# A decoder trunk's first output projection: its first pair of chunks with a quarter of the contraction in seven products

## The chip, the cores and the metric

The kernel runs on one core of one Trainium2 chip. The metric is the device time of one execution in microseconds: the median of 3 runs is 1020.32 us (1020.16 to 1020.44).

The engines are named as in the profile: PE is TensorE (matmuls), PEld its loading of the stationary operand, DVE is VectorE, ACT is ScalarE, POOL is GpSimd, SP is SyncE. SP and POOL issue the DMAs that matter here, each in the order of its own queue. A name with q behind it (SPq, POOLq) is the engine's instruction queue.

## The reference

Two layers over 256 positions of 2048 features in fp32. The first layer runs two token mixers side by side and projects their gated outputs back to 2048 features. That projection is the subject:

```python
ya = hgrn2(...)
ya = head_rmsnorm(ya, a_norm[j]) * jax.nn.silu(za.astype(jnp.float32))
xc = causal_conv(xb, b_conv_w[j], b_conv_b[j])
yb = rg_lru(xc, ...)
yb = yb * jax.nn.silu(zb.astype(jnp.float32))
y = jnp.concatenate([ya, yb], axis=-1).astype(h.dtype)
mix = y @ e_w_out[j]
...
h = h + mix
pl = rmsnorm(p[i].astype(h.dtype) @ ple_w[i], ple_norm[i])
h = h + jax.nn.sigmoid(h @ ple_gate_w[i]) * pl
```

y is 256 x 2048 and e_w_out is 2048 x 2048.

## The kernel before

**Products.** Every large product is made in three matmuls. Weights are loaded in blocks of 128 x 1024 floats (512 KB), and each block is split into a high part (a cast on ACT to fp32r, L137 or L221) and a low part (a subtraction on DVE, L138 or L222). Activations are split the same way. One step of 128 features of the contraction is then hi by hi, hi by lo and lo by hi, each a matmul of 128 x 128 against 128 x 512. The two halves of the positions (128 each, called hf) have a PSUM bank each.

**Chunks and quarters.** A projection's 2048 output features are cut into four chunks of 512, and the contraction into four quarters (kq) of 512. One quarter of one chunk is two weight blocks and 24 matmuls, 12 for each half. `quarter_tok` does this straight. In the first output projection (weights `a["eo"]`), `project_two` makes chunks 0 and 1 side by side in the order (chunk, quarter) (0,0) (0,1) (1,0) (1,1) (0,2) (1,2) (0,3) (1,3), in four banks.

**Seven products.** `seven` makes a pair of chunks, with one quarter of the contraction as a two by two product of blocks in seven products (Strassen's scheme in Winograd's form): products over half a quarter, 6 matmuls each, instead of eight. It needs four combinations of activations (`combos`, kept in tiles q4 and named 1 to 4), and combinations of weight blocks. These come about in three tiles: X (chunk 0, first half of the quarter), Y (chunk 1, second half) and Z (chunk 0, second half), to which the fourth block (chunk 1, first half) is added. With `acc` the fourth block is added by accumulating DMAs from POOL's queue (`add_loaded`): into X once X has been split, into Y once Y has been split and added to X. Without it the block is loaded once and DVE adds it. Banks A and F collect the halves of the first chunk, E and B those of the second; two partial sums, b5 and g, lie in SBUF. The order is a string: digits are products, a and b a straight quarter of the first or second chunk (`plain`), a dot a `pump` of waiting side work, A and F hand a half on. Products 1 and 3 (X straight, Y with combination 4) stood ahead of the string. The second pair of this projection (chunks 2 and 3) is made with `seven` in the order a5a6.2aA7b.4F.bb, without `acc`.

**Buffers.** Straight blocks go through a ring of five tiles `raw`, the split parts through four pairs whi and wlo, so a cast waits until the matmuls of the split four earlier are done. X, Y and the partial sums of a pair lie in a pool of the stage: the mixers' pool is `m0`, and pool `e0` takes its place in memory when `m0_scope.close()` is called. Before, that is after the first half of chunk 0 has been handed on (`mixed`). Anything in e0 waits for the last use of what lay in m0.

**Side work.** y comes in eight tiles, two for each quarter, by generators: `feature_major` for the first half of the features, `gated_mix` for the second, of which the last comes from the last gate chunk (weights `ew`, chunk 7). A gate chunk is transposed on DVE (L699), written to DRAM and read back in another order by POOL's queue (`across`, tiles dzb and r), and then multiplied with the mixer's output (L1048) and split. `before(kq)` runs such a generator to its end ahead of the quarter that needs it. The residual h (tiles hq) is loaded by POOL's queue; `out_proj` adds each half of a chunk to it (L604).

**Order.** The program text and priorities given to some instructions set the order on each engine when the kernel is built. Each engine runs its own list in order and waits on semaphores.

## Time and profile before

| | |
|---|---|
| median of 3 runs | 1020.32 us (1020.16 to 1020.44) |
| time of the profiled execution | 1020.23 us |
| its span in the profile | 1018.4 us |
| mean granted TensorE clock | 0.998 |
| last gate chunk ends, first output projection begins on PE | 300.01 us from the span's start |
| its second pair of chunks begins on PE | 343.53 us |

The span is the part of the execution that the profile covers; 1.8 us of the execution lie around it. Times in the profile are counted from the span's start. A group of instructions is one line, engine, operation and kind of tile, as in `L222 DVE TENSOR_TENSOR wlo<-ch,whi`, and a row of the timeline gives start, duration, engine, line, operation, tiles and count; what stands in brackets is the engine's idle time just before and what ended it. A matmul's modelled duration, 0.39 us, reaches over its successor's start, so the distance of two starts is what one matmul costs.

### The profile page before, as it was taken

The numbers are of one execution on the slowest core, as the hardware profiler recorded it, in microseconds if no ns is written. First come the engines' busy times: TensorE is split into PE (matmuls) and PEld (weight loads), VectorE is DVE, ScalarE is ACT, GpSimd is POOL, SyncE is SP. The second block draws the span as 40 slices with busy tenths as digits, with TensorE's granted clock in tenths as the row PEclk, the third lists the DMA queues.
The fourth block names the chain that finished last, engine by engine and source line by source line (L and its number), as shares of the span: only waits on it lengthen the run. The fifth ranks groups of instructions, "written<-read, shape, count | busy, mean of one in ns | idle before, by whom it ended". The sixth has DMA issues, their size and how long they took to land.

```text
span 1018.4 us, 14515 instructions
## 1 busy us (share of the span) xinstructions
PE 1009.4 (99%) x5158; PEld 838.1 (82%) x5158; DVE 842.8 (83%) x1234; ACT 661.4 (65%) x949; POOL 101.3 (10%) x182
## 2 busy tenths in 40 slices
PE   9999999999999999999999999999999999999996
PEld 8888888888888888888888888888888888888886
DVE  7858969969687887898669997888889997999794
ACT  7675554686875554666557877776676777466562
POOL 0111101011111112021011100000011110102000
PEclk9999999999999999999999999999999999999999
DMA  9987756567778799487798757567879889696852
GB/s 364 330 233 240 225 177 197 166 204 225 251 235 305 238 315 291 155 284 249 258 337 250 228 166 227 166 208 201 256 193 283 233 249 356 181 288 217 279 186 83
DMA packets 69816, 242.66 MB, mean 238 GB/s; under 512 B 9040, under 2 KB 10448, under 8 KB 69744
## 3 DMA queue, kind: packets, MB, share of 16 engines
q1 hardware_dynamic: 56016, 198.08, 58.7%
q0 software_dynamic: 13296, 43.13, 16.1%
q8 instruction: 40, 0.66, 0.3%
q10 hardware_dynamic: 432, 0.52, 0.1%
q14 instruction: 32, 0.26, 0.1%
HBM read 221.78 MB, written 19.92 MB: 237 GB/s over the span
## 4 chain that ended last, share of the span: by engine, by line
PE 99%; ACT 0%; DMA 0%; issue 0%; DVE 0%; ACTq 0%; POOLq 0%
PE mm L235 29%; PE mm L211 14%; PE mm L212 14%; PE mm L213 14%; PE mx L235 8%; PE mx L211 3%; PE mx L212 3%; PE mx L213 3%; PE mm L517 1%; PE nu L1349 1%; PE mx L517 1%; PE mm L1562 1%; PE mm L1561 1%; PE mm L1563 1%; PE st L213 1%; PE st L235 1%
## 5 line engine op out<-in xcount | busy, mean ns | idle before, releaser
L137 ACT CAST whi<-raw 128x1024 fp32r<-128x1024 f32 (+1 forms) x309 | 322.6, 1047 | 211.3 <-PE mm L213 95.2
L138 DVE TENSOR_TENSOR wlo<-raw,whi 128x1024 fp32r<-128x1024 f32 (+1 forms) x309 | 371.6, 1213 | 104.0 <-ACT whi L137 97.8
L211 PE MATMUL mm<-whi,ahl 128*128 128x512 f32 x640 | 250.5, 392 | 0.0
L212 PE MATMUL mm<-wlo,ahl 128*128 128x512 f32 x640 | 249.4, 390 | 0.0
L213 PE MATMUL mm<-whi,ahl 128*128 128x512 f32 x640 | 249.3, 389 | 0.0
L235 PE MATMUL mm<-whi,ahl 128*128 128x512 f32 x720 | 231.8, 390 | 0.0
L235 PEld LDWEIGHTS mm<-whi,ahl 128*128 128x128 f32 x720 | 135.2, 188 | 27.9
L211 PEld LDWEIGHTS mm<-whi,ahl 128*128 128x128 f32 x640 | 120.2, 188 | 25.5 <-issue 0.4
L213 PEld LDWEIGHTS mm<-whi,ahl 128*128 128x128 f32 x640 | 120.2, 188 | 25.1
L235 PE MATMUL mm<-wlo,ahl 128*128 128x512 f32 x360 | 140.5, 390 | 0.0
L212 PEld LDWEIGHTS mm<-wlo,ahl 128*128 128x128 f32 x640 | 120.2, 188 | 24.3
L222 DVE TENSOR_TENSOR wlo<-ch,whi 128x1024 fp32r<-128x1024 f32 x67 | 81.1, 1221 | 12.5 <-ACT whi L221 11.1
L221 ACT CAST whi<-ch 128x1024 fp32r<-128x1024 f32 x67 | 70.1, 1050 | 26.8 <-PE mm L235 13.8
L235 PEld LDWEIGHTS mm<-wlo,ahl 128*128 128x128 f32 x360 | 67.6, 188 | 14.1 <-DVE wlo L222 0.3
L235 PE MATMUL mx<-whi,ahl 128*128 128x512 f32 x192 | 63.3, 390 | 0.0
L212 PE MATMUL mx<-wlo,ahl 128*128 128x512 f32 x128 | 49.8, 389 | 0.0
L213 PE MATMUL mx<-whi,ahl 128*128 128x512 f32 x128 | 49.8, 389 | 0.0
L211 PE MATMUL mx<-whi,ahl 128*128 128x512 f32 x128 | 49.8, 389 | 0.0
L235 PE MATMUL mm<-whi,q 128*128 128x512 f32 x144 | 49.1, 391 | 0.0
L235 PEld LDWEIGHTS mx<-whi,ahl 128*128 128x128 f32 x192 | 36.1, 188 | 7.9 <-ACT xr L575 0.4
L235 PE MATMUL mx<-wlo,ahl 128*128 128x512 f32 x96 | 37.4, 390 | 0.0
L235 PEld LDWEIGHTS mm<-whi,q 128*128 128x128 f32 x144 | 27.0, 188 | 5.7
(389 smaller groups left out, 1318.5 us busy)
## 6 DMA issues: line engine op xcount, KB each, us to landing
raw<-in_ew_dram SPq DMA_DIRECT2D x64, 512.0 KB, 5.2
raw<-in_g_dram SPq DMA_DIRECT2D x60, 512.0 KB, 4.5
raw<-in_oqk_dram SPq DMA_DIRECT2D x32, 512.0 KB, 5.5
raw<-in_eo_dram SPq DMA_DIRECT2D x30, 512.0 KB, 5.1
raw<-in_oo_dram SPq DMA_DIRECT2D x30, 512.0 KB, 6.4
raw<-in_ov_dram SPq DMA_DIRECT2D x29, 512.0 KB, 4.2
raw<-in_oog_dram SPq DMA_DIRECT2D x24, 512.0 KB, 4.1
raw<-in_oz_dram SPq DMA_DIRECT2D x20, 512.0 KB, 5.1
```

The lines of the kernel that those rows point to most:

```text
L137: last["act"] = s.copy(h, r).ins
L138: last["dve"] = v.tensor_tensor(out=l, in0=r, in1=h.bitcast(F32), op=ALU.subtract).ins
L211: te.matmul(ps[hf], xh, wh, start=(k == 0), stop=False, skip_group_check=True)
L212: te.matmul(ps[hf], xh, wl, start=False, stop=False, skip_group_check=True)
L213: last["pe"] = te.matmul(ps[hf], xl, wh, start=False, stop=(k == KT - 1), skip_group_check=True).ins
L221: last["act"] = s.copy(hi, r).ins
L222: last["dve"] = v.tensor_tensor(out=lo, in0=r, in1=hi.bitcast(F32), op=ALU.subtract).ins
L235: last["pe"] = te.matmul(o, x, y, start=(first and k + i == 0), stop=(end and k == n - 1 and i == 2), skip_group_check=True).ins
L517: last["pe"] = te.matmul(ps[hf][:, o:o + w_], tokens(pact[x], k, hf), (hi, lo)[y][:, k * 512 + o:k * 512 + o + w_], start=(n == mine[0]), ...
L1349: te.matmul(ps[:, 0:n], x[:, i, o:o + P], y[:, b, i], start=(b == 0 and x is sh and y is vh), stop=(b == hf and y is vl))
L1561: te.matmul(o, xh, wh, start=(k == 0), stop=False)
L1562: te.matmul(o, xh, wl, start=False, stop=False)
```

## The change

The first pair of the first output projection (chunks 0 and 1) goes through `seven` instead of `project_two`, with the order 3a5a6.27ba4AF.bb and with `acc`. The combinations of the first quarter are started before the last two gate chunks instead of at the projection's start, and the same q4 tiles serve both pairs. X and Y of the first pair take tiles of m0 (tag f) and the partial sums another (tag q); m0 is closed, and e0 opened, when the first pair is through. Product 3 becomes a letter of the order strings, and so does the third chunk's quarter of another stage (c); the orders of all other stages stay as they were. The new function `moved` has no caller.

```diff
-ORDERS = {1: "a5a6.2aA7b.4F.bb", 2: "a5.2aA64.7F.bb"}
-LATE = "a526.a7b4aAF.bb"
+ORDERS = {1: "3a5a6.2aA7b.4F.bb", 2: "3a5.2aA64.7F.bb"}
+LATE = "c3a526.a7b4aAF.bb"
...
-    def two_and_seven(w, act, before, where, places, home=None, begin=None):
-
-        qs = {}
-        start("combos", combos(act, 0, qs, *where))
-        for c, ps in enumerate(project_two(w, act, before)):
-            for hf in range(2):
-                yield c, hf, ps[hf]
+    def two_and_seven(w, act, before, where, places, home=None, begin=None, first=None, qs=None):
+
+        if first is not None:
+            drain("combos")
+            yield from seven(w, 0, act, qs, (0,), *first(), order="3a5a6.27ba4AF.bb", acc=True, before=before)
+        else:
+            qs = {}
+            start("combos", combos(act, 0, qs, *where))
+            for c, ps in enumerate(project_two(w, act, before)):
+                for hf in range(2):
+                    yield c, hf, ps[hf]
         drain("combos")
         if begin is not None:
             begin()
...
-        if third is not None:
-            plain(w, j + 2, kqs[0], act, third, (True, True))
-        Y = load(room, 1, 1)
-        product(E, combo(4), split(Y), home is None)
-        W = X
-        if not acc:
-            W = load(ring, 1, 0)
-            add(Y, W)
-            add(W, X)
         did = set()
         for op in order or ORDERS[len(kqs)]:
-            if op in "ab":
+            if op == "c":
+                plain(w, j + 2, kqs[0], act, third, (True, True))
+            elif op == "3":
+                Y = load(room, 1, 1)
+                product(E, combo(4), split(Y), home is None)
+                W = X
+                if not acc:
+                    W = load(ring, 1, 0)
+                    add(Y, W)
+                    add(W, X)
+            elif op in "ab":
...
             combine()
+        qsy = {}
+        start("combos", combos(y, 0, qsy, ap, "ahl"))
         for g in range(2):
             ps = project_tok(ew, 6 + g, acth)
...
     def mixed():
-        for c, hf, src in two_and_seven(a["eo"], y, ready(y, "fm"), (ap, "ahl"), in_e0):
+        for c, hf, src in two_and_seven(a["eo"], y, ready(y, "fm"), None, in_e0, None, in_m0_end, in_m0, qsy):
             if hf == 0 and c in (1, 2):
                 load_hq(c + 1, last["hop"])
-            if (c, hf) == (0, 0):
-                m0_scope.close()
-                pe0.append(l0.enter_context(tc.tile_pool(name="e0", bufs=1)))
             yield c, hf, src
+
+    def in_m0():
+        return (lambda: m0.tile([P, 1024], F32, name="ch", tag="f"),
+                pieces(m0.tile([P, 1536], F32, name="pr", tag="q")[:, 0:1024]))
+
+    def in_m0_end():
+        m0_scope.close()
+        pe0.append(l0.enter_context(tc.tile_pool(name="e0", bufs=1)))
```

POOL's queue from the last gate chunk's way through DRAM on, before. dzb1 is that chunk in DRAM and r its way back, hq the residual, wg a tile of the later stage, dfe0 the way of chunk 0's result:

```order
L686 DMA dzb1_3051<-w_3047 128x1024
L689 DMA r_3050<-dzb1_3051 32x4x256 x4
L1111 DMA hq_3057<-in_x_dram 128x2x512
L1111 DMA hq_3059<-in_x_dram 128x2x512
L1141 MEMSET wg_3777 128x512
L686 DMA dfe0_3363<-w_3359 128x1024
```

The same queue now. ch_3082 is X of the first pair and ch_3097 its Y:

```order
L331 DMA ch_3082<-in_eo_dram 128x1024
L704 DMA dzb1_3067<-w_3063 128x1024
L707 DMA r_3066<-dzb1_3067 32x4x256 x4
L1131 DMA hq_3073<-in_x_dram 128x2x512
L1131 DMA hq_3075<-in_x_dram 128x2x512
L331 DMA ch_3097<-in_eo_dram 128x1024
L704 DMA dfe0_3338<-w_3334 128x1024
```

Two accumulating DMAs are new: the one into X stands ahead of the gate chunk's way through DRAM, the one into Y behind it and behind both loads of the residual.

SP's queue around the first loads of the second pair, before, with the semaphores that each waits for (DMAHW and DMASW are transfers issued by SP and by POOL, DVE and PE the engines). ch_3424 and ch_3438 are X and Y of the second pair, in e0:

```order
L134 DMA raw_3375<-in_eo_dram 128x1024 [waits DMAHW0_49,DVE_49]
L297 DMA raw_3450<-in_eo_dram 128x1024 [waits DMAHW1_49,DVE_49]
L297 DMA ch_3424<-in_eo_dram 128x1024 [waits DVE_49,PE_49]
L297 DMA ch_3438<-in_eo_dram 128x1024
L134 DMA raw_3454<-in_eo_dram 128x1024 [waits DMAHW2_49,DVE_49]
L134 DMA raw_3460<-in_eo_dram 128x1024 [waits DMAHW3_49,DVE_49]
```

The same place now; X and Y of the second pair are ch_3440 and ch_3454:

```order
L134 DMA raw_3386<-in_eo_dram 128x1024 [waits DMAHW7_49,DVE_49]
L314 DMA raw_3466<-in_eo_dram 128x1024 [waits DMAHW0_49,DVE_49]
L134 DMA raw_3470<-in_eo_dram 128x1024 [waits DMAHW1_49,DVE_49]
L134 DMA raw_3476<-in_eo_dram 128x1024 [waits DMAHW2_49,DVE_49]
L134 DMA raw_3518<-in_eo_dram 128x1024 [waits DMAHW3_49,DVE_49]
L134 DMA raw_3524<-in_eo_dram 128x1024 [waits DMAHW4_49,DVE_49]
L314 DMA ch_3440<-in_eo_dram 128x1024 [waits DMASW6_49,DVE_49,PE_49]
L314 DMA ch_3454<-in_eo_dram 128x1024
L1164 DMA gr_3791<-in_ogf_dram 128x256
L314 DMA raw_3575<-in_eo_dram 128x1024 [waits DMAHW6_49,DMAHW5_49,DVE_49]
```

X and Y of the second pair moved behind four blocks of the second pair's straight quarters. X's load now also waits for a transfer of POOL's queue, the accumulation into the first pair's Y, and the DVE instruction that it waits for is another: before it was the last multiply of `gated_mix`, now it is the sum of the residual with the first half of chunk 1 in `out_proj`, which reads the partial sum g in m0.

More of the change, by code (lines that the diff above doesn't have):

```diff
@@ L247, in plain, with moved, known @@
                 pump()
+    def moved(qs, kq, pool, tag):
+        for q, names in qs["tiles", kq]:
+            t = pool.tile([P, 1024], F32R, name="q4", tag=tag)
+            s.copy(t, q.bitcast(F32))
+            known(qs, kq, t, names)
+            yield
+    def known(qs, kq, q, names):
+        for n, name in enumerate(names):
+            qs[name, kq] = [[q[:, i * 512 + n * T + k * P:i * 512 + n * T + (k + 1) * P] for k in range(2)]
+                            for i in range(2)]
     def combos(act, kq, qs, pool, tag, bufs=None, offset=0):
@@ L268, in keep @@
                 v.tensor_tensor(out=q[:, 512:1024], in0=c, in1=q[:, 0:512].bitcast(F32), op=ALU.subtract)
-            for n, name in enumerate(names):
-                qs[name, kq] = [[q[:, i * 512 + n * T + k * P:i * 512 + n * T + (k + 1) * P] for k in range(2)]
-                                for i in range(2)]
+            known(qs, kq, q, names)
+            qs.setdefault(("tiles", kq), []).append((q, names))
         while 2 * kq + 1 not in act:
```

## The prediction

> **What bounds the kernel now.** I read the page first, then the stage that the change touches in a table of windows, then who issues what there on each queue.
>
> ```profile
> span 1018.4 us, 14515 instructions
> PE 1009.4 (99%) x5158; PEld 838.1 (82%) x5158; DVE 842.8 (83%) x1234; ACT 661.4 (65%) x949; POOL 101.3 (10%) x182
> ...
> PE 99%; ACT 0%; DMA 0%; issue 0%; DVE 0%; ACTq 0%; POOLq 0%
> ```
>
> TensorE is the chain: 99% of it, and no other engine has a share. A matmul taken away is gained, and any wait of TensorE is paid in full, since nothing later is idle to absorb it. The windows of the first output projection (columns: busy us and instructions of PE, PEld, DVE, ACT, POOL, then clock, DMA share, GB/s) say the same:
>
> ```profile
> 264.00:272.00 8.00, 8.00 (x40) 6.74 (x39) 3.50 (x3) 7.96 (x16) 2.19 (x4) 1.00 0.62 188
> ...
> 304.00:312.00 8.00, 8.00 (x37) 6.63 (x36) 7.19 (x11) 5.47 (x7) 3.41 (x6) 1.00 0.83 279
> 312.00:320.00 8.00, 8.00 (x37) 6.61 (x36) 4.87 (x6) 2.92 (x4) 0.76 (x2) 1.00 1.01 325
> ```
>
> TensorE is busy 8.00 us of 8 with the full clock, while the DMA engines are at their limit around 312 to 320. So the question is whether the new order of work keeps TensorE fed.
>
> **What is taken away.** The timeline of TensorE gives the first matmul of this projection and the first one of its second pair:
>
> ```profile
> 300.01 0.39 PE L211 MATMUL mm<-whi,ahl 128*128 128x512 f32 x1
> ...
> 343.53 0.39 PE L235 MATMUL mm<-whi,ahl 128*128 128x512 f32 x1
> ```
>
> Between them lie 192 matmuls (two chunks, four quarters, 24 each), so one takes 43.52 / 192 = 0.2267 us. In the changed first pair one quarter goes as seven products of 6 instead of 48 matmuls: 6 fewer, **-1.36 us**. If TensorE stayed fed the pair would end at 300.01 + 186 x 0.2267 = 342.18.
>
> **What costs nothing.** A split is a cast on ACT and a subtraction on DVE, in the page's groups (count, then busy us and mean ns):
>
> ```profile
> L222 DVE TENSOR_TENSOR wlo<-ch,whi 128x1024 fp32r<-128x1024 f32 x67 | 81.1, 1221 | 12.5 <-ACT whi L221 11.1
> L221 ACT CAST whi<-ch 128x1024 fp32r<-128x1024 f32 x67 | 70.1, 1050 | 26.8 <-PE mm L235 13.8
> ```
>
> Three more splits, two sums of the same shape on DVE (I take 1.2 us each) and seven copies and sums of banks come into a stage where ACT and DVE have room: they are busy 2.92 and 4.87 us of 8 in the window 312 to 320. Without that room they would cost up to 8 us, DVE's share. The combinations, moved up by some 30 us, add to DVE where it has 3.50 us of 8; ACT, full there, gets two short casts. A cast leads its matmuls by several us, which covers this: the timeline shows one that had to wait 3.02 us for a weight buffer.
>
> ```profile
> 293.41 1.05 ACT L137 CAST whi<-raw 128x1024 fp32r<-128x1024 f32 x1 [3.02 <-PE mm L213]
> ...
> 294.49 2.59 DVE L138 TENSOR_TENSOR wlo<-raw,whi 128x1024 fp32r<-128x1024 f32 x2 [1.60 <-ACT whi L137]
> ```
> ```profile
> ch<-in_ov_dram POOLq DMA_DIRECT2D x2, 512.0 KB, 6.6
> ```
>
> That cast is now the one of the first tile, X, whose split is done near 296. The accumulation into X stands on POOL's queue ahead of the last gate's bounce and can go then; POOL idles 15.32 us before 304.60 (below), so it delays nobody. X is needed again after 36 matmuls, at 308.2; 296 plus 6.6 us as in the same step of in_ov plus a split of 2.3 us is 304.9, hidden by 3 us.
>
> **The first new wait: the second accumulation.** The seven-product order of this pair is 3 a 5 a 6 2 7: product 7 comes after 78 matmuls, at 300.01 + 78 x 0.2267 = 317.69. It needs tile Y with the second chunk's weights accumulated into it, by a DMA on POOL's queue. That DMA now stands behind the last gate's bounce to DRAM, its four reads back and two loads of the residual. From before:
>
> ```profile
> 301.51 0.69 DVE L1099 SCALAR_TENSOR_TENSOR u<-th,u 128x512 f32<-128x512 f32 x1 [0.18 <-ACT u L1098]
> ...
> 303.59 0.70 DVE L699 STREAM_TRANSPOSE w<-u 128x512 f32<-128x512 f32 x1
> ```
> ```profile
> 304.60 0.56 POOL L686 DMA_DIRECT2D dzb<-w  x1 [15.32 <-DVE w L699]
> 309.15 2.18 POOL L689 DMA_DIRECT2D r<-dzb  x4 [3.99 <-DMA dzb<-w]
> 311.32 1.44 POOL L1111 DMA_DIRECT2D hq<-in_x_dram  x2
> ```
>
> The transpose waited behind a combination and a split; the combinations are gone from there now, so it can follow the gate's product at once: 302.9. The bounce goes out 0.3 us later (304.29 to 304.60), the reads 4.55 us after it, then 2.18 and 1.44 us of issuing: the accumulation is issued near **311.4**. How long it takes to land is not shown for this place; the nearest rows are:
>
> ```profile
> hq<-in_x_dram POOLq DMA_DIRECT2D x4, 512.0 KB, 9.0
> ```
> ```profile
> DMA to landing us min/median/max: 5.5/6.8/10.0
> ```
>
> The second row is that of the eight accumulations of in_oz on this queue, the same size. I take 9.0, since it goes third in a row of 512 KB transfers while the DMA engines are full: landed at 320.4. A cast of 1.05 us and a subtraction of 1.22 us, with 0.1 us ahead of the cast, follow, so the second matmul of product 7 (the first that needs the low part) runs at 322.8 instead of 317.9: **+4.9 us**. With 5.5 us to landing it is 1.4, with 10.0 it is 5.9. Queued behind it on TensorE is everything; DVE and ACT, in order, hold the next splits behind Y's.
>
> **The second new wait: the first load of the second pair.** Its X lies in pool e0, which lies where m0 lay. Before, m0 was closed after the first chunk and its last reader was the multiply with tt:
>
> ```profile
> 324.20 1.29 DVE L1048 TENSOR_TENSOR xr<-r,tt 128x512 f32<-128x512 f32 x2
> ```
> ```profile
> 325.56 0.81 SPq L297 DMA_DIRECT2D ch<-in_eo_dram  x2
> ```
>
> It ends at 325.49 and the load goes 0.07 us later, 18 us ahead of its use at 343.53. Now the first pair's own X, Y and partial sums lie in m0, and m0 closes when the pair is through; the load waits for the last of them, the residual's sum with the partial sum of chunk 1. That sum needs bank E, whose last matmul stands only 12 from the pair's end, at 339.46 (plus the first wait). The same step at the end of before's second pair shows the latencies:
>
> ```profile
> 382.97 0.39 PE L235 MATMUL mm<-whi,ahl 128*128 128x512 f32 x1
> ```
> ```profile
> 383.28 0.68 DVE L318 TENSOR_TENSOR pr<-mx,pr 128x512 f32<-128x512 f32 x1
> 383.88 0.68 DVE L253 TENSOR_TENSOR xr<-ahl 128x512 f32<-128x512 f32 x1
> 384.48 0.69 DVE L604 TENSOR_TENSOR hq<-pr,hq 128x512 f32<-128x512 f32 x1
> ```
>
> E's sum starts 0.31 us after the bank is done (339.77), the next DVE step 0.60 later (340.37), ends at 341.06; SP issues at 341.2. The landing of exactly this load:
>
> ```profile
> DMA to landing us min/median/max: 4.4/5.2/6.0
> ```
>
> With 5.2 it lands at 346.4, is cast by 347.55 and split by 348.8; the second matmul runs at 348.85 instead of 342.41: **+6.4 us** (5.6 to 7.3). Then Y's split, two sums and the splits of the next quarter queue on DVE at 1.15 us each, five of them within 12 matmuls: by that row the fifth is late by 0.5 us (0 to 1), **+0.5 us**. On SP behind the waiting load stand Y, a small load and Z and the later quarters; the two quarters used first are ahead of it, so nothing else starves.
>
> **The clock.** Before has no stop of TensorE, so no row shows one inside. Its end does:
>
> ```profile
> 1010.04 0.28 PE L1563 MATMUL mm<-whi,ahl 128*128 128x256 f32 x1
> ```
> ```profile
> 1012.00:1013.00 1.00, 0.00 (x0) 0.00 (x0) 0.78 (x6) 0.50 (x4) 0.00 (x0) 1.00 0.00 0
> 1013.00:1014.00 1.00, 0.00 (x0) 0.00 (x0) 1.00 (x4) 0.72 (x1) 0.00 (x0) 0.69 0.00 0
> 1014.00:1015.00 1.00, 0.00 (x0) 0.00 (x0) 0.41 (x2) 0.51 (x1) 0.00 (x0) 0.50 0.74 256
> ```
>
> The granted clock (last column but two) goes to 0.50 near 1013.4, 3.1 us after the last matmul. Both new stops are longer (3.8 us and 5.3 us to their first matmul). How long the clock then stays down no row shows; I take as long as it took to fall, 3.1 us at half speed, 1.55 us lost each time, an estimate, with 0 as the lower end, and count it for one stop of the two: **+1.55 us**. [...]
>
> **The sum.** Profiled execution 1020.23 (span 1018.4 and 1.8 around it, 0.09 below the median 1020.32, which I neglect): 1020.23 - 1.36 + 4.9 + 6.4 + 0.5 + 1.55 = 1032.2, said as **1032 us**, slower.
>
> **The rivals.**
> - Both stops, and the clock falls in both: + 1.55, 1033.8. For it: both are longer than 3.1 us. Against: one fall alone is seen, and the first stop is longer by only 0.7 us.
> - Both stops with the clock held: 1030.7.
> - Only the second stop: the accumulation lands 5 us earlier than I say, within 4 us of issue, or it is issued earlier. 5.5 us is the shortest that its like took, which still leaves 1.4 us. Then 1020.23 - 1.36 + 6.9 = 1025.8, up to 1027.3 with the clock.
> - Only the first stop: X of the second pair is not held by m0. For it: its address is that of the first pair's Y, not of the partial sums. Against: before, it waited for a tile elsewhere in m0. 1023.8, to 1025.3.
> - The other side, not slower: both waits are hidden, and six matmuls are all that changes: 1018.9, faster by 0.13%, which is no difference that a measurement of this kernel can tell (about 0.2%). The point at which this decides is the issue of two DMAs: the accumulation before some 306, and the second pair's first load before some 334. Nothing in the queues lets either go so early.
> - The change doesn't do what it says: excluded as far as the program shows, since the pair has 186 matmuls.
> - A third stop: the pieces of y for the third quarter come late, now that they are needed after 42 matmuls, at 309.5, instead of after 96. In before the last of them was made at 312.7:
>
> ```profile
> 287.09 2.18 POOL L689 DMA_DIRECT2D r<-dzb  x4 [4.16 <-ACT xr L717]
> ```
> ```profile
> 312.00 0.68 DVE L152 TENSOR_TENSOR ahl<-xr,ahl 128x512 fp32r<-128x512 f32 x1
> ```
>   Against: its data were read back from 287.09 on and there by some 297, and DVE merely took it late. Late by 1 to 3 us: to 1035.
>
> **How the numbers follow.** One stop's clock counted with both stops 0.34; both clocks 0.18; none 0.15; only the second stop 0.17; only the first 0.06; neither 0.05; a third stop besides 0.05. Likeliest 1032. The low end takes 1.4 and 5.6 us with no clock and no queueing (1025.9) and so holds the case without the first stop; the high end 5.9, 7.3, 1.0 and twice 1.55 (1036.2): 1025.5 to 1037. That leaves out the case of no wait, part of the first-only case, and the worst of the third stop. Slower by over 0.2% 0.94, within 0.2% 0.05, faster 0.01.
>
> **What would show it.** In the changed profile, TensorE's chain should lose share to two places: a wait of some 4 to 5 us before product 7 near 318 for Y's cast, with POOL's accumulation issued near 311; and one of 5 to 6 us before the second pair's first product near 347, with SP's load issued some 1 us before the first pair's last matmul. The granted clock should be below 1.00 in the few us behind at least one of them. The prediction is wrong if POOL's accumulation is issued before 306, if SP's load goes before the first pair's last 24 matmuls, or if TensorE shows no idle time above 1 us between 300 and 360.

## The result, and the profile after

| | before | after |
|---|---|---|
| median of the runs, us | 1020.38 (6 runs, 1019.86 to 1022.35) | 1039.1 (6 runs, 1037.93 to 1040.5) |
| ratio to before | 1 | 1.0182, 95% interval 1.0169 to 1.0195 |
| the profiled execution, its span, us | 1020.23, 1018.4 | 1039.82, 1038.0 |
| mean granted clock | 0.998 | 0.991 |

The change makes the kernel slower by 18.7 us. The prediction had the sign and two of the places, but 7 us too little: 1032, and the time lies above its range. Medians are over all runs and ratios over the fast ones, and only e17_four below and the kernel before beside it had one slow run each (1121 and 2636 us). The page of the changed kernel answers to the first rows shown of before:

```profile
span 1038.0 us, 14524 instructions
PE 1014.5 (98%) x5152; PEld 839.9 (81%) x5152; DVE 851.7 (82%) x1242; ACT 665.2 (64%) x956; POOL 103.3 (10%) x184
...
PE 93%; DMA 3%; ACT 1%; DVE 1%; issue 1%; POOL 0%; ACTq 0%; POOLq 0%; SPq 0%; DVEq 0%
```

TensorE's share of the chain fell from 99% to 93%; a DMA now has 3%, most of it loads of `in_eo`. TensorE is busy for 5 us longer with six matmuls fewer, which is for the most part the clock (5.3 us, below). The list of TensorE's waits names what ended them (total us, times, longest):

```profile
PE mm L239 <- ACT whi L225: 9.7, 2, 5.1
PE mm L239 <- ACT mm L362: 2.1, 1, 2.1
PE mm L239 <- DVE wlo L226: 1.2, 2, 0.8
```

The prediction had two stops; there are three. Their rows in TensorE's timeline, each behind the last matmul ahead of it or, for the second, alone (its last matmul ahead starts at 321.03):

```profile
302.84 0.39 PE L239 MATMUL mx<-whi,q 128*128 128x512 f32 x1
305.30 0.50 PE L239 MATMUL mm<-whi,ahl 128*128 128x512 f32 x1 [2.07 <-ACT mm L362]
...
307.75 0.50 PE L239 MATMUL mm<-wlo,ahl 128*128 128x512 f32 x1 [0.57 <-DVE wlo L138]
...
326.48 0.79 PE L239 MATMUL mm<-whi,q 128*128 128x512 f32 x1 [5.06 <-ACT whi L225]
327.74 0.80 PE L239 MATMUL mm<-wlo,q 128*128 128x512 f32 x1 [0.47 <-DVE wlo L226]
...
354.11 0.39 PE L239 MATMUL mm<-whi,ahl 128*128 128x512 f32 x1
359.14 0.50 PE L239 MATMUL mm<-whi,ahl 128*128 128x512 f32 x1 [4.65 <-ACT whi L225]
360.40 0.80 PE L239 MATMUL mm<-wlo,ahl 128*128 128x512 f32 x1 [0.76 <-DVE wlo L226]
```

A matmul fed follows the one ahead by 0.227 us. So the first stop costs 305.30 - 302.84 - 0.23 = 2.2 us and 0.7 more at 307.75; the second, to the low part, 327.74 - 321.49 = 6.25; the third 360.40 - 354.57 = 5.83. Then the granted clock, in windows of 1 us (the last column but two):

```profile
325.00:326.00 1.00, 0.00 (x0) 0.00 (x0) 0.00 (x0) 0.62 (x1) 0.00 (x0) 0.81 0.00 0
...
332.00:333.00 1.00, 1.00 (x5) 0.78 (x5) 1.00 (x2) 0.00 (x0) 0.00 (x0) 0.78 0.81 279
...
359.00:360.00 1.00, 0.50 (x1) 0.19 (x1) 0.87 (x1) 0.09 (x1) 0.00 (x0) 0.88 1.15 208
...
366.00:367.00 1.00, 1.00 (x4) 0.76 (x4) 1.00 (x2) 0.00 (x0) 1.00 (x3) 0.71 0.62 234
```

It is 0.50 from 325.6 to 332.4 and from 359.8 to 366.6, each 6.8 us. Between the low parts and the return of the clock 12 and 15 matmuls take 5.02 and 6.40 us instead of 2.72 and 3.40: 2.3 and 3.0 us lost. The account of the 19.6 us between the two spans:

| | us |
|---|---|
| the projection starts later (300.35 instead of 300.01, from the kernel's first loads) | +0.3 |
| six matmuls fewer | -1.4 |
| first stop, at the pair's start | +2.9 |
| second stop, product 7 | +6.25 |
| third stop, the second pair's start | +5.8 |
| half clock behind the second and the third | +2.3 + 3.0 |
| sum | 19.2 |

What stood ahead of the first stop shows in the rows of SP, DVE and ACT:

```profile
288.38 2.29 DVE L1056 TENSOR_TENSOR_SCAN tt<-av,it 128x1024 f32<-128x1024 f32 x1
290.74 0.33 SPq L314 DMA_DIRECT2D ch<-in_eo_dram  x1
298.51 1.05 ACT L225 CAST whi<-ch 128x1024 fp32r<-128x1024 f32 x1 [3.71 <-DMA ch<-in_eo_dram]
...
301.39 0.69 ACT L1117 ACTIVATE th<-mm,rth 128x512 f32<-128x512 f32 x1
...
304.64 0.61 ACT L362 COPY mm<-mm 128x512 f32<-128x512 f32 x1
```

Y lies where the scan's operand lay, so its load goes out at 290.74, behind the scan, and lands 7.7 us later. ACT works in order and stands 3.71 us idle in front of Y's cast; behind it stand the last gate's tanh (297.49 before, 301.39 now) and the copy of bank A to bank F, without which TensorE may not go on in F at 303.07. The second stop's rows: the accumulation was issued at 315.57, not 311.4, and landed near 325.3.

```profile
315.57 0.94 POOL L331 DMA_DIRECT2D ch<-in_eo_dram  x1
325.38 1.04 ACT L225 CAST whi<-ch 128x1024 fp32r<-128x1024 f32 x1 [3.93 <-DMA ch<-in_eo_dram]
```

The third's: the last reader of the first pool ends at 353.23, SP issues at once, X lands some 4.7 us later.

```profile
352.54 0.69 DVE L622 TENSOR_TENSOR hq<-pr,hq 128x512 f32<-128x512 f32 x1
353.29 0.80 SPq L314 DMA_DIRECT2D ch<-in_eo_dram  x2
358.05 1.04 ACT L225 CAST whi<-ch 128x1024 fp32r<-128x1024 f32 x1 [13.34 <-DMA ch<-in_eo_dram]
```

### The profile page after: what moved, and what is told of

Same layout as the page of the kernel before. It is cut to its first block, busy times and chain, and to the rows that moved or that the text cites. A ratio compares the mean times of both kernels' runs of the same rounds, so it can differ in the third digit from the quotient of the medians.

```text
span 1038.0 us, 14524 instructions
## 1 busy us (share of the span) xinstructions
PE 1014.5 (98%) x5152; PEld 839.9 (81%) x5152; DVE 851.7 (82%) x1242; ACT 665.2 (64%) x956; POOL 103.3 (10%) x184
## 4 chain that ended last, share of the span: by engine, by line
PE 93%; DMA 3%; ACT 1%; DVE 1%; issue 1%; POOL 0%; ACTq 0%; POOLq 0%; SPq 0%; DVEq 0%
PE mm L239 30%; PE mm L215 13%; PE mm L216 13%; PE mm L217 13%; PE mx L239 9%; DMA ch<-in_eo_dram 2%; PE mx L217 2%; PE mx L215 2%; PE mx L216 2%; PE mm L535 1%; PE nu L1374 1%; PE mx L535 1%; PE mm L1587 1%; PE mm L1588 1%; PE mm L1586 1%
## 5 line engine op out<-in xcount | busy, mean ns | idle before, releaser
L137 ACT CAST whi<-raw 128x1024 fp32r<-128x1024 f32 (+1 forms) x305 | 317.7, 1046 | 192.8 <-PE mm L217 83.7
L138 DVE TENSOR_TENSOR wlo<-raw,whi 128x1024 fp32r<-128x1024 f32 (+1 forms) x305 | 366.4, 1212 | 88.6 <-ACT whi L137 82.6
L216 PE MATMUL mm<-wlo,ahl 128*128 128x512 f32 x608 | 236.7, 389 | 0.0
L239 PEld LDWEIGHTS mm<-whi,ahl 128*128 128x128 f32 x804 | 151.8, 189 | 38.9 <-ACT whi L225 5.1
L239 PE MATMUL mm<-wlo,ahl 128*128 128x512 f32 x402 | 157.6, 392 | 1.3 <-DVE wlo L226 0.8
L215 PEld LDWEIGHTS mm<-whi,ahl 128*128 128x128 f32 x608 | 114.1, 188 | 24.2 <-issue 0.4
L217 PEld LDWEIGHTS mm<-whi,ahl 128*128 128x128 f32 x608 | 114.1, 188 | 23.8
L225 ACT CAST whi<-ch 128x1024 fp32r<-128x1024 f32 x73 | 76.3, 1050 | 52.6 <-DMA ch<-in_eo_dram 22.3
L226 DVE TENSOR_TENSOR wlo<-ch,whi 128x1024 fp32r<-128x1024 f32 x73 | 88.4, 1221 | 25.1 <-ACT whi L225 23.4
L239 PE MATMUL mx<-whi,ahl 128*128 128x512 f32 x216 | 71.9, 394 | 0.0
L239 PE MATMUL mm<-whi,q 128*128 128x512 f32 x156 | 54.4, 398 | 5.1 <-ACT whi L225 5.1
L239 PEld LDWEIGHTS mx<-whi,ahl 128*128 128x128 f32 x216 | 41.3, 191 | 9.1 <-ACT xr L593 0.4
L239 PE MATMUL mx<-wlo,ahl 128*128 128x512 f32 x108 | 42.6, 394 | 0.0
L215 PE MATMUL mx<-whi,ahl 128*128 128x512 f32 x96 | 37.3, 389 | 0.0
L216 PE MATMUL mx<-wlo,ahl 128*128 128x512 f32 x96 | 37.3, 389 | 0.0
L217 PE MATMUL mx<-whi,ahl 128*128 128x512 f32 x96 | 37.3, 389 | 0.0
```

Of the source, the lines that this page charges most:

```text
L137: last["act"] = s.copy(h, r).ins
L138: last["dve"] = v.tensor_tensor(out=l, in0=r, in1=h.bitcast(F32), op=ALU.subtract).ins
L215: te.matmul(ps[hf], xh, wh, start=(k == 0), stop=False, skip_group_check=True)
L216: te.matmul(ps[hf], xh, wl, start=False, stop=False, skip_group_check=True)
L217: last["pe"] = te.matmul(ps[hf], xl, wh, start=False, stop=(k == KT - 1), skip_group_check=True).ins
L225: last["act"] = s.copy(hi, r).ins
```

## The experiments

Theory: three stops, each with its own cause, and the half clock behind two of them, make the whole of it; the seven products and the combinations themselves cost nothing. Rival theories: the combinations push back the gate; the stops hang on DVE's and ACT's order in any case, so that taking one cause away only moves the wait; the clock is a by-product without a price. Times are medians, beside runs of the kernel before on the same chip (1020.1 to 1020.7 us).

### The combinations alone

`e6_combos` is the kernel before with the combinations started under the last gate chunks and the old first pair.

```diff
+        qsy = {}
+        start("combos", combos(y, 0, qsy, ap, "ahl"))
         for g in range(2):
             ps = project_tok(ew, 6 + g, acth)
```

> The kernel before, with one part of the change alone: the combinations are formed under the last gate chunks; the first pair stays as it was (192 matmuls). Theory: all the time comes from the seven products' waits and none from the combinations: 1020.5 us, within 0.2%, and no wait of TensorE above 0.5 us between 290 and 360. Rival: the combinations on DVE and ACT push back the gate, the bounce and the pieces of y (the changed kernel's read back was issued at 289.52 instead of 287.09) and so make part of the first stop: 1021.5 to 1023.

1020.5 us, ratio 1.0000 (0.9991 to 1.0010). The combinations cost nothing, and the rival that they push the gate back falls. Everything is in the seven products.

### The first stop: Y's cast on ACT

`e1_y_early` gives Y the place of a tile last read at 215.56.

```diff
-                Y = load(room, 1, 1)
+                Y = load(room2 or room, 1, 1)
...
+        room2=lambda: m0.tile([P, 1536], F32, name="chq", tag="q")[:, 0:1024])
```

> The changed kernel, but Y of the first pair lies in the place of an earlier tile (the convolved input of the first half, last read at 215.56), so that its load no longer waits for the scan. Theory: the stop of 3.2 us at the pair's start came from ACT, which stood in order behind Y's cast (3.71 us idle for Y's load); with Y early the copy of bank F is in time and that stop goes. The gate's product and the bounce are some 4 us earlier too, so the accumulation into Y is issued near 311.5 instead of 315.57 and the stop before product 7 keeps its length (5 to 5.5 us) but begins 3 us earlier: 1039.1 - 3.2 = 1036 us. Rival: the accumulation's landing is set by something else (the transfers then in flight), it lands at 325 all the same, the second stop grows by what the first one loses, and the time stays at 1039.

1037.83 us, ratio 1.0168 (1.0148 to 1.0189): less than half of the expected gain. (The mean granted clock of the profiled execution is 0.993 here and 0.991 in the changed kernel.) Y's cast is at 295.06, but ACT then stood for the next thing in its order, the split of the third quarter's pieces of y, which waits for a product on DVE with data read back through DRAM:

```profile
298.13 0.62 ACT L151 CAST ahl<-xr 128x512 fp32r<-128x512 f32 x1 [2.02 <-DVE xr L1067]
300.06 0.69 ACT L1118 ACTIVATE th<-mm,rth 128x512 f32<-128x512 f32 x1
...
303.98 0.50 PE L240 MATMUL mm<-whi,ahl 128*128 128x512 f32 x1 [0.79 <-ACT mm L363]
306.42 0.50 PE L240 MATMUL mm<-wlo,ahl 128*128 128x512 f32 x1 [0.56 <-DVE wlo L138]
```

`e7_gate` orders that split behind the gate's copies as well.

```diff
+                with ExitStack() as behind:
+                    if j == 0:
+                        behind.enter_context(tc.issue_after(through[1]))
...
+                    y[4 + 2 * j + b] = split_act(x, "y")
```

> e1_y_early (Y's load early), and besides the product and the split of the third quarter's pieces of y are ordered behind the last gate's copies on ACT, where in e1_y_early that cast waited 2.02 us for the read back and held the gate's tanh until 300.06. Theory: ACT's order is the whole of the first stop; with both casts out of the way tanh runs near 297.5 as before, bank F is copied in time and the stop (3.2 us changed, 1.7 us in e1_y_early) is gone: 1037.8 - 1.7 = 1036.1, and with the accumulation issued some 2.5 us earlier the second stop is shorter by up to 0.8: 1035.3 to 1036.1. Rival: the pieces of y are then late for the third quarter's products (needed some 42 matmuls in), a new wait there, and no gain: 1037.8.

1036.41 us, ratio 1.0151 (1.0136 to 1.0167), as the theory said: tanh at 297.66, the copy of F at 301.79, and of the stop one short wait is left.

```profile
297.66 0.69 ACT L1122 ACTIVATE th<-mm,rth 128x512 f32<-128x512 f32 x1 [0.37 <-PE mm L218]
...
301.79 0.57 ACT L363 COPY mm<-mm 128x512 f32<-128x512 f32 x1
...
305.14 0.50 PE L240 MATMUL mm<-wlo,ahl 128*128 128x512 f32 x1 [0.49 <-DVE wlo L138]
```

So the first stop is ACT's order: two casts whose data come late, ahead of a copy for which TensorE waits. It is worth 2.7 us. The second stop did not shrink with it: the accumulation goes out 2.9 us earlier (312.68), is there near 323.4 (10.7 us instead of 9.7), and product 7 is earlier too.

### The second stop: the accumulation into Y

`e2_ring` takes the accumulations off POOL's queue: SP loads the block, DVE adds it.

```diff
-            yield from seven(w, 0, act, qs, (0,), *first(), order="3a5a6.27ba4AF.bb", acc=True, before=before)
+            yield from seven(w, 0, act, qs, (0,), *first(), order="3a5a6.27ba4AF.bb", acc=False, before=before)
```

> The changed kernel, but the second chunk's weights are not accumulated by DMA: they are loaded to the ring by SP and added on DVE (two more sums of 1.2 us, no transfer on POOL's queue). Theory: the stop before product 7 is the accumulation's (issued at 315.57 behind the bounce, landed near 325); without it the stop of 5.4 us, the wait of 1.0 us for the low part, and the half clock behind it (4.6 us left of 6.8, so 2.3 us lost) go: about 1039.1 - 8.5 = 1030.6 us. The first stop stays (3.2 us), and so does the one at the second pair. Rival: POOL's queue is not what counts, DVE and ACT come to Y's split only near 325 in their order anyhow: no change, 1039. Second rival: with one more block in the ring of five the loads fall behind, and a new stop eats part: 1033 to 1036.

1031.93 us, ratio 1.0108 (1.0092 to 1.0125). The stop before product 7 is gone with its half clock: its matmuls start 0.23 us apart, from 322.88 on. The 1.3 us to the expectation are the first stop, which grew: 3.3 and 1.4 us instead of 2.2 and 0.7. Y's cast came 0.4 us later (298.87), and the sums on DVE stand ahead of the split that TensorE waits for next.

`e9_order` leaves the accumulation where it is and moves product 7 two straight quarters back. (There the second chunk's first quarter is summed into bank B ahead of product 7's subtraction, so the second half of the first chunk gets another sum than the reference's; the work is the same in number and kind.)

```diff
-order="3a5a6.27ba4AF.bb"
+order="3a5a6.2ba74AF.bb"
```

> The changed kernel with product 7 two straight quarters later in the first pair (3a5a6.2ba74AF.bb instead of 3a5a6.27ba4AF.bb): 48 matmuls, 10.9 us, more for the accumulation into Y to land; nothing else. Theory: the second stop (5.2 us to the first product, 1.0 us to the low part) and its half clock (2.2 us by e4_fill) go, as they did with the ring in e2_ring, at no cost on DVE: 1039.1 - 8.4 = 1030.7 us; the first and the third stop stay. Rival: the quarters put ahead need pieces of y (the last quarter's, from the bounce) that are no earlier than the accumulation, and TensorE waits for those instead: 1035 to 1039.

1031.12 us, ratio 1.0098 (1.0085 to 1.0111): the theory's number within 0.4 us, by another way than the ring. Together with e2_ring, which has no such transfer, this shows that the wait is for that one transfer and not for a place in DVE's or ACT's order.

### What the half clock costs

In three kernels TensorE does matmuls in the waits whose result nobody reads.

```diff
+            elif op == "7":
+                if third is None and order:
+                    padded(act, 22)
                 product(B, combo(3), split(Y))
```

> The changed kernel with the waits left as they are, but TensorE kept at work in two of them: 22 matmuls of the same shape (4.99 us) on a bank that nothing reads go ahead of product 7, and 20 (4.53 us) ahead of the second pair. Theory: the half clock behind each stop (6.83 us in the granted clock's record) is caused by TensorE's idleness and costs 2.3 us and 3.05 us beyond the waits; with the idle time filled the clock stays at 1.00 and the time falls by 5.4 us to 1033.7. By my prediction's term (1.55 us in all) it would fall to 1037.6. Rival: what TensorE loses behind the stops is the splits queued on DVE, not the clock: 1039 as before, with the clock full.

1044.9 us, ratio 1.0237 (1.0215 to 1.0259), not what was expected: the code put the 20 matmuls in a second place too, the same step of the last layer's output projection (they run there from 899.96 to 904.50, 4.5 us), and the total says nothing. The stretch behind the second stop does. From the low part of product 7 to bank E's sum it is 351.81 - 327.74 = 24.07 us in the changed kernel and 349.75 - 327.90 = 21.85 here, at the full clock. First the changed kernel's matmuls, then the same ones of e4_fill:

```profile
330.04 0.63 PE L239 MATMUL mx<-whi,ahl 128*128 128x512 f32 x1
330.46 0.63 PE L239 MATMUL mx<-wlo,ahl 128*128 128x512 f32 x1
```
```profile
329.15 0.39 PE L240 MATMUL mx<-whi,ahl 128*128 128x512 f32 x1
329.38 0.39 PE L240 MATMUL mx<-wlo,ahl 128*128 128x512 f32 x1
```

They stand 0.42 us apart in the one and 0.23 in the other.

> The changed kernel with its waits as they are and TensorE kept at work in the second and third stop, with matmuls on a bank that nothing reads: 22 (4.99 us) ahead of product 7, 25 (5.67 us) ahead of the second pair, 10 (2.27 us) between the second pair's first and second product; none elsewhere. Theory (the clock): in e4_fill the stretch from product 7's low part to bank E's last sum took 349.75 - 327.90 = 21.85 us instead of 351.81 - 327.74 = 24.07 us, so 2.2 us of the changed kernel's time is the half clock of the second stop; the third one's 6.83 us at half clock cost about 3 us more. With both filled the clock stays at 1.00 throughout and the time falls by 5.2 us, to 1034. Rival (the short waits behind a stop, for low parts and for Y, are what costs, and they hold the clock down in any case): the second stop alone gains, 1036.9. Second rival (splits queue, no clock): 1039.

1038.98 us, ratio 1.0181 (1.0164 to 1.0198), not what was expected, though the granted clock was 1.00 behind both stops (326 to 330 and 356 to 364) and 0.998 in the mean. The filling itself is the reason in part: behind the third stop the half clock had hidden the wait for Y, which the ten matmuls between the products into banks A and E replace (E's begins at 362.15, at 362.70 in the changed kernel). From the low part (358.60) to product 5 (368.95) the stretch is 10.35 us; in the changed kernel, from 360.40 to 371.35, it is 10.95, and the profiled execution is 2.4 us shorter than the changed kernel's (1037.4 and 1039.82). Two of its four runs took 1040 us all the same; why is not settled. So of the 3.0 us of half clock behind the third stop this filling gained only 0.6 while Y comes as late as it does.

> The changed kernel with 22 matmuls (4.99 us) on a bank that nothing reads ahead of product 7, and no other filling. Theory: the wait stays as it is, the clock stays at 1.00 behind it, and the time falls by the 2.2 us that the profiles of e4_fill and e5_fill show in this stretch: 1036.9 us. Rival: the filling is a cost of its own, or the stop behind it takes the gain back (the second pair's start waits for a load that is issued by the last sum, which moves with the matmuls, so it should not): 1039.

1036.61 us, ratio 1.0160 (1.0146 to 1.0174), with the filling ahead of product 7 alone: 2.5 us less than the changed kernel, as expected. The wait is the same to 0.2 us (the low part comes 6.9 us after the start of the last matmul ahead, 6.7 in the changed kernel), the stretch to bank E's sum is 349.15 - 327.30 = 21.85 us again. The profiled execution is 3.3 us shorter than the changed kernel's (1036.53 and 1039.82), since its first and third stops are shorter too, by 0.5 and 0.9. That the clock has a price of its own, 2.2 us here, is shown.

### The third stop: the first pool's close

`e12_gate_order` is `e7_gate` with the order of `e9_order` (and its other sums): the first two stops are taken away and the third is left.

> e7_gate (first stop gone) with the order of e9_order (second stop gone): the third stop is left alone. Theory: the stops are independent and add up, so 1020.4 - 1.4 + 9 (5 us to the first product, 1.0 to the low part, 3 of half clock) = 1028 us, with one fall of the granted clock, of 6.83 us, near 350. Rival: the stops fed on each other (one stop gave DVE and ACT time to get ahead), the third grows, and the time is 1030 or more.

1028.27 us, ratio 1.0067 (1.0050 to 1.0084). The three stops add up, and the third alone is worth 1028.3 - (1020.7 - 1.4) = 9 us with its clock. Taking it away was harder. `e3_room` puts the second pair's tiles into the first pool and closes it after that pair.

```diff
+    def in_m0_more():
+        return (lambda: m0.tile([P, 1024], F32, name="ch", tag="k"),
+                pieces(m0.tile([P, 1536], F32, name="pr", tag="q")[:, 0:1024]))
...
     act = out_proj(hq, mixed(), "fe")
+    in_m0_end()
```

> The changed kernel, but the second pair's X, Y and partial sums lie in other tiles of the first pool (the places of the two scans' outputs and of the other convolved input), and that pool is closed after the second pair. Theory: the stop at the second pair's start is the load of X, which waits for the pool's last reader at 353.2; loaded in advance, the stop (4.8 us to the first product, 1.0 us more to the low part) and the half clock behind it (6.1 us, so 3.05 lost) go: 1039.1 - 8.9 = 1030.2 us. Rival: the loads of X and Y, now ahead of the quarters' blocks on SP's queue, hold those up and a new wait of 1 to 3 us appears: 1031 to 1033. Second rival: closing the pool later delays the next stage's loads: the same size there.

1035.48 us, ratio 1.0146 (1.0129 to 1.0164): the stop at the second pair is gone and its clock with it (the pair's matmuls start 0.23 us apart from 354.78 on), but there are two new waits of the size that the rivals gave. The second has the cause that was named, the first another.

```profile
361.21 0.58 ACT L363 ACTIVATE mm<-mm 128x512 f32<-128x512 f32 x1 [2.39 <-DVE hq L622]
361.85 0.50 PE L239 MATMUL mm<-whi,ahl 128*128 128x512 f32 x1 [1.47 <-ACT mm L363]
...
423.22 2.50 DVE L577 TENSOR_TENSOR pl<-pl,row 128x512 f32<-128x512 f32 x4 [5.68 <-DMA row<-in_rows_dram]
...
427.77 0.50 PE L216 MATMUL mx<-wlo,ahl 128*128 128x512 f32 x1 [1.48 <-DVE wlo L138]
```

The last sum of the residual now stood on DVE behind the splits of the pair that had come early, and held a bank; and the gain's row, in the second pool, came late in the next stage, with DVE in order behind it.

> e3_room (third stop taken away, the other two left) with the residual's sums ahead on DVE and the gain's row given three steps more. Theory: the third stop and the half clock behind it are worth 9.2 us (e12_gate_order), and e3_room's 1035.5 fell short of that by its two new waits (1.62 and 1.64 us) and a second stop longer by 1.1 us: here about 1039.1 - 9.2 + 1 = 1031 us, no wait of TensorE above 0.5 us after 334. Rival: the close of the pool after the second pair delays more than the row (the gate's weights, the combinations' tiles), and the wait moves on to them: 1034 or more.

1038.18 us, ratio 1.0170 (1.0155 to 1.0186), not what was expected. The residual's sums with priority cured the first wait. Three steps more for the row did not cure the second: the four products with it moved together and stood 8.78 us in front of the row's transfer, and TensorE waited 3.71 us at 427.83. `e16_room_sp` has SP load the row as soon as the pool is closed.

```diff
-    start("pg", ple_gain(pls, lambda: row(e0, "row", 2, 0)))
+    start("pg", ple_gain(pls, lambda: [half_row(e0, "row", 2, 0, b, sy) for b in range(2)]))
```

> e3_room (third stop alone taken away) with the residual's sums ahead on DVE and the gain's row loaded by SP, ahead of the next stage's blocks, instead of by POOL behind the last reads. Theory: no wait near 427 any more; the third stop's 9.2 us go, less the 1 us by which the second stop is longer without it: 1031 us. Rival: the row on SP's queue holds up two blocks of the next stage, and the wait is theirs: 1033 to 1036.

1032.94 us, ratio 1.0123 (1.0110 to 1.0137): 6.2 us less than the changed kernel, no wait behind 334, and 1.9 us above the expectation. Of this the profiled execution lost 1.6 us at the kernel's first weights, which the edit does not touch: its pair starts at 301.93, at 300.35 in the changed kernel. The first stop, of the same length as in the changed kernel (2.08 and 2.07 us), brought the clock down to 0.50 here. That cost little in the end, as the half clock hid the wait for the next low part and the second stop was shorter (4.32 us idle ahead of its first product, 5.06 in the changed kernel): product 7's low part comes 1.6 us later as well (329.32 and 327.74).

```profile
306.88 0.79 PE L239 MATMUL mm<-whi,ahl 128*128 128x512 f32 x1 [2.08 <-ACT mm L362]
```
```profile
306.00:307.00 1.00, 0.12 (x1) 0.12 (x1) 1.00 (x2) 1.00 (x3) 0.00 (x0) 0.95 0.22 86
...
310.00:311.00 1.00, 1.00 (x5) 0.83 (x4) 1.00 (x2) 0.70 (x2) 0.00 (x0) 0.85 1.09 348
```

### All remedies together

Five kernels join the remedies, to see whether the six matmuls show once nothing waits. (`e10_best` too has the order and the sums of `e9_order`.)

> All remedies together: Y loaded early, the third quarter's split behind the gate's copies, ring block and sums on DVE instead of the two accumulations, the second pair's tiles in the first pool, and the residual's sums ahead in DVE's order (in e3_room one of them stood behind nine sums and splits of the next products, and bank B with it: 1.62 us). Theory: the stops, the half clock behind them and nothing else made the changed kernel slow; without them remain six matmuls fewer: 1020.5 - 1.4 = 1019.1 us, up to 1020.8 if the wait of 1.64 us for the gain's row near 427, seen in e3_room, stays. Rival: a ring of five blocks and DVE's order hold less work in advance than the quarters did, and new waits of 2 to 5 us appear in this stage: 1022 to 1025, slower than before.

> e12_gate_order with the second pair's tiles in the first pool and the residual's sums ahead on DVE (third stop gone), and the gain's row given two steps more before DVE's products with it (in e8_all those stood in DVE's order 7.08 us for the row and cost TensorE 3.1 us near 412). Accumulations stay on POOL, the ring is not used for them. Theory: nothing is left but the six matmuls: 1019.1 us, 0.13% under the kernel before, the same within the measurement. Rival: e8_all's spread (1023.3 to 1031.6) comes from something else than the ring, waits for loads in the next stage, because the first pool closes later: 1022 to 1026, slower than before.

> e10_best with product 7 one straight quarter later instead of two (3a5a6.2a7b4AF.bb, which keeps the outputs) and the gain's row given three steps more instead of two. Theory: 1019.1 us, six matmuls under the kernel before, up to 1020.5 with short waits left: the same within the measurement. Rival 1: the third quarter's products, now ahead of product 7, wait for the last pieces of y (their cast was at 317.87 in e7_gate, where they would be needed at 318.9), one wait of 1 to 2 us: 1021. Rival 2: later closing costs more than the row, as above: 1022 to 1024.

> e13_best (no first, second and third stop) with the gain's row loaded by SP. Theory: 1019.1 to 1020.5 us, within 0.2% of the kernel before: the seven products gain six matmuls once their tiles are in time. Rival: loads of the next stage are late in one place or another as long as the pool closes later: 1022 to 1026.

> e15_row_sp with the order 3a5a6.24a7bAF.bb instead of 3a5a6.2a7b4AF.bb: product 4 (6 matmuls, 1.36 us) goes ahead of the last quarter's products, which in e15_row_sp waited 1.19 us and then 0.35 us for pieces of y near 319 and were followed by a window of 3.41 us at half clock. Theory: those two waits and the half clock (1.35 + 0.52 + up to 1.7 us) were all that was left: 1023.8 - 3.5 = 1020.3 us, or 1019.1 if the six matmuls show, the same as before within the measurement. Rival: the split of X for product 4, now needed some 20 us earlier, is not there (its sum with Z comes after Z's load), and the wait moves to product 4: 1022 to 1024.

| kernel | us | ratio to before | longest wait left (profiled execution) |
|---|---|---|---|
| e8_all, ring | 1025.69 | 1.0059 (1.0041 to 1.0077) | 2.92 at 412, the gain's row |
| e10_best, accumulation | 1023.68 | 1.0027 (1.0014 to 1.0040) | 2.51 at 419, the row |
| e13_best, order 2a7b4 | 1027.91 | 1.0070 (1.0053 to 1.0087) | 3.27 at 418, the row |
| e15_row_sp | 1023.84 | 1.0031 (1.0019 to 1.0043) | 1.19 at 319, the last pieces of y |
| e17_four | 1022.31 | 1.0018 (1.0008 to 1.0027) | 1.71 at 324, the low part of those pieces |

None reached 1019.1; the expectations of this part were all too low, by 2 to 8.8 us. The theory's account holds in so far as the three stops are absent from all five, but for short waits: e10_best has two of 0.5 and 0.8 us in the first one's place. The longest waits left are those of the table. Behind them the granted clock was 0.50 for 3.4 us in e15_row_sp, and in e13_best the matmuls start 0.43 us apart (418.26 to 419.97) instead of 0.23. (They are from one execution each; e10_best's, of 1027.61 us, was the slowest of its eleven.) The rival, that the rows and pieces of the neighbouring steps come onto the path next, holds as well. The best, `e17_four`, is still slower than the kernel before by 0.18%, so no version was found that is faster; whether 1019.1 can be had is open. Its profiled execution was 2.35 us behind the kernel before when the first weights were used up (18.84 and 16.49 us), a place that none of the remedies touch. That this explains some of the spread of its runs is likely and not shown.

## Why the prediction was wrong

- **What bounds the kernel** (right). A wait of TensorE is paid in full, and nothing later gave any of the 19 us back.
- **What is taken away** (right). -1.36 us; the account closes to 0.4 us with it.
- **What costs nothing** (wrong, and the step that failed first). "A cast leads its matmuls by several us, which covers this" was argued for the matmuls that use the cast. I followed X's cast through ACT's order and not Y's, whose load stands behind the scan on a place that becomes free at 290.67. ACT, in order, passed the late cast on to what stood behind it: the gate's tanh (301.39 instead of 297.49) and the copy of bank F. e1_y_early and e7_gate show it: 2.7 us. The combinations did cost nothing (e6_combos), and X's accumulation was hidden.
- **The third-stop rival** had the right tile and the wrong place. I asked whether the third quarter's pieces of y would be late for TensorE; they were in time for it, but their split held up ACT's order (2.02 us in e1_y_early).
- **The first new wait** (mechanism right, size 1.35 us short: 6.25 for 4.9). The issue was 4.2 us later than 311.4, because the transposes stand behind the tanh that stop 1 delayed (2.9 of the 4.2, by e7_gate), while TensorE was ready for product 7 only 3.6 us later (321.26 for 317.69); and the landing took 9.7 us and not 9.0. e2_ring and e9_order take it away in two ways, for 7.2 and 8.0 us with its clock.
- **The second new wait** (right: 5.8 for 6.4, the landing was 4.7 us and not 5.2). SP's load went 0.8 us ahead of the pair's last matmul, where some 1 us was written. The 0.5 us for DVE's queue are not seen apart from the half clock.
- **The clock** (wrong, the largest term). I took 3.1 us at half speed at one stop, "as long as it took to fall". It fell at both, 4.2 and 5.3 us after the last matmul's end, and stayed down for 6.8 us each time: 5.3 us lost instead of 1.55. The time to the fall, 3.1 us in the kernel before and 4.2 and 5.3 here, did not give the time that it stayed down. e11_fill7 shows 2.2 us of it by itself. The case that had both clocks counted both at 3.1 us and so was no bound.

In sum, over the prediction (the second stop's size, the first stop, the clock, the third stop without the 0.5, the later start): 1.35 + 2.9 + 3.75 - 1.1 + 0.3 = 7.2 of the 7.6 us between 1032.2 and the profiled 1039.82.

## What to carry to other kernels

Where a change puts a transfer's data in front of an engine that works in order, list everything that stands behind the first instruction to need it, not only its own users; the first victim here was a copy that had nothing to do with the new tile. A place in a shared pool decides when a load may go, and moving the pool's close moves the wait to what the next pool holds. And two of the three stops of TensorE had two prices here, their lengths (6.25 and 5.8 us) and the half clock behind them (2.3 and 3.0 us more).

## What the runs showed of the hardware

- **Where the clock fell in this stage it stayed at 0.50 for 6.8 or 3.4 us.** In the changed kernel the granted clock falls to 0.50 at 325.62 and 359.75 and is back at 1.00 at 332.44 and 366.58, 6.8 us later each time. Worked out from windows of 1 us it was down from 305.70 to 309.12 in e9_order (0.85 in 305 to 306, 0.94 in 309 to 310), from 306.90 to 310.30 in e16_room_sp and from 321.04 to 324.44 in e15_row_sp: 3.4 us each time. What makes it the one or the other is not shown.
- **The length of a stop alone did not decide whether the clock fell.** A first stop of 2.07 us left it at 1.00 in the changed kernel and one of 2.08 brought it down in e16_room_sp. Two waits of 3.15 and 1.22 us in e2_ring left the matmuls behind them 0.23 us apart (306.82 to 307.52, and from 309.69 on), as at the full clock, and in e15_row_sp two waits of 1.19 and 0.35 us brought it down:

```profile
319.12 0.50 PE L240 MATMUL mm<-whi,ahl 128*128 128x512 f32 x1 [1.19 <-ACT ahl L151]
320.21 0.73 PE L240 MATMUL mm<-whi,ahl 128*128 128x512 f32 x2 [0.35 <-DVE ahl L152]
```
```profile
321.00:322.00 1.00, 1.00 (x3) 0.50 (x2) 0.56 (x1) 0.41 (x1) 0.00 (x0) 0.52 1.01 316
...
324.00:325.00 1.00, 1.00 (x4) 0.79 (x4) 0.00 (x0) 0.01 (x1) 0.00 (x0) 0.78 1.02 414
```

  What does decide was not tried and is not shown.
- **The same 512 KB took between 4.7 and 10.7 us to land.** The load of the second pair's X took 4.7 us, that of Y 7.7, the accumulation into Y 9.7 and, issued 2.9 us earlier in e7_gate, 10.7; the two halves of the gain's row took 7.9 and 9.9 us in the kernel before, 8.3 and 10.3 in the changed one. For the accumulation, earlier issue was worth less than its lead: product 7 began 1.9 us earlier (324.56 and 326.48). What sets the time, queue, kind of transfer or the transfers beside it, was not tried.
